# Seven block products in place of eight for two pairs of column chunks in each of ten gated FFNs

## The chip, the cores and the metric

One core of a Trainium2 chip runs the whole program. The metric is device time in microseconds (us), the median of the runs. The engines are named as in the profile: PE is TensorE (matrix products; PEld are its weight loads), DVE is VectorE, ACT is ScalarE, POOL is GpSimd, and SP is SyncE, whose queue issues the large transfers from DRAM. Each engine runs its own queue of instructions in order, and waits at an instruction whose inputs, or whose destination buffer, are not free yet.

## The reference

A network of 256 tokens with 1024 features, all in float32: four layers of FFN, attention, FFN, and then two layers of a mixer and an FFN. What the change touches are the ten FFNs, eight of the first kind and two of the second (`modulate` scales and shifts by columns of a small product with `w_ada`):

```python
D_MODEL = 1024; SEQ = 256; DEPTH = 4; DEPTH_2 = 2; D_FF = 2816

def swiglu(x, w_in, w_out):
    gate, up = jnp.split(x @ w_in, 2, axis=-1)
    return (jax.nn.silu(gate) * up) @ w_out

h = h + 0.5 * rms_norm(swiglu(rms_norm(h, g[0]), ffn_w_in[i, 0], ffn_w_out[i, 0]), g[1])
...
mod = c_act @ w_ada[l] + b_ada[l]
```

The weights of the FFNs come from DRAM in float32, and each is used once.

## The kernel before, in words

**Products.** A float32 value is split into two float32r parts, hi and lo. `hilo` does it: ACT casts a tile to hi (line 168) and DVE subtracts hi from the tile to give lo (line 169). `mm3` then takes a product as three PE matmuls of 128x512, xh·wh, xh·wl and xl·wh (lines 217, 219, 221), accumulated in a PSUM bank. `weights` loads a raw tile of 128x2048 (1 MB) on SP's queue (line 179) and splits it in two halves of 128x1024. There are 2 raw buffers (`RAW_BUFS`) and 9 buffers each for hi and lo (`W_BUFS`).

**An FFN.** The tokens are two tiles of 128 (t = 0, 1), the 1024 features are 8 k-tiles, and the 2816 hidden columns are 11 chunks of 256. `f1(c, t)` takes chunk c's gate and up columns side by side (512 columns): four hi/lo pairs per chunk, and per token tile a *first product* of 8 k-tiles × 3 = 24 matmuls. `hidden` then makes the hidden values: tanh on ACT (line 411), two DVE operations (lines 413 and 414) into the tile `hd`, and two PE transposes (line 249), whose result ACT and DVE split again into `hT` (lines 261, 262). `f2(c, t)` multiplies `hT` with chunk c's rows of `w_out` (two hi/lo pairs, 12 matmuls of 128x512) and accumulates in the banks `aA` or `aB`. A chunk is thus 48 + 24 matmuls of 128x512 on PE, and six hi/lo pairs on ACT and DVE.

**Order.** `ffn` issues the first products of chunks 0 and 1, and then for each chunk c two first products and the second products of chunk c − 2. `middle` (after chunk 3) loads the gain of the norm, or in the second block starts a task that sums a gate (`gbc`). After each of chunks 4 to 7 `ada_step` adds 256 rows of `w_ada`, weighted, to a tile `ada`: four DVE operations of 128x512 on a raw tile of its own, `araw` (lines 1027, 1029). Chains that hop between engines are generators, which are continued when a clock counted in matmuls reaches their time; the list of instructions that comes of this is then put on the engines' queues by the framework's scheduler, once and for all, when the program is built.

In the text the FFNs are numbered #1 to #10 in order of time, and *the stretch* of an FFN runs from the end of its fourth first product (chunks 0 and 1 for both token tiles) to the start of the first product of chunk 8. Chunks 2 to 7 lie in it, so both changed pairs do.

Of the kernel before, what the change touches and what calls it, by code (L numbers as in the profile page):

```python
# [37 lines left out]
W_BUFS = 9  # L38
# [3 lines left out]
GATE_STEP = 9.0  # L42

# [56 lines left out]
class _Net:  # L100
# [63 lines left out]
    # A float32 value is the exact sum of two float32r parts, hi and lo.  x @ w is taken as  # L164
    # xh @ wh + xh @ wl + xl @ wh, accumulated in float32.
# [75 lines left out]
    def last_steps(self, acc, steps):  # L241
        """steps: (hT, ws); one half of the columns after the other"""
# [8 lines left out]
    def to_hT(self, nat, scale=None):  # L251
        """[128 tok, 256] -> (hi, lo) [128, 2, 128 tok]."""
# [16 lines left out]
    def setup(self):  # L269
# [13 lines left out]
        def columns(src, rows, eng=nc.sync):  # L283
            """DRAM [rows, 128] -> [128, rows]."""
# [21 lines left out]
    def mean_square(self, halves, a0, a1):  # L306
        """a0 + a1 * the sum of squares of two [128, 512]; a1 is a number, a0 a number or [128, 1]"""
# [56 lines left out]
    def post_norm(self, t, acc, g_bc, a=1.0, eps=EPS):  # L364
        """h += acc * (a * mean square of acc + eps) ^ -1/2 * g"""
# [17 lines left out]
    def prepare(self, n, t):  # L383
        """Starts what the next part of the network needs of a token tile."""
# [12 lines left out]
    def ffn(self, w_in, w_out, factors, finish, middle):  # L397
        """factors(t): r / 2 and r^2 for x's factor r, which x^T lacks; finish(t, acc) takes the
        accumulated product, in which the hidden values are r^2 (1 + tanh(r g / 2)) g u."""
# [30 lines left out]

        first = ((0, 0), (0, 1), (1, 0), (1, 1)) if self.stage == 0 else ((0, 0), (1, 0), (0, 1), (1, 1))
        for c, t in first:
            f1(c, t)
        for c in range(2, NCH):
            for t in range(NT):
                f1(c, t)
                if c < NCH - 1:
                    f2(c - 2, t=t)
            if c == 3:
                middle()  # L440
            elif self.stage > 0 and c in (4, 5, 6, 7):
                self.ada_step()
# [4 lines left out]
        self.drain()  # L447

    def ffn_1(self, li, j):
# [14 lines left out]
        self.ffn(self.a["ffn_w_in"][li, j], self.a["ffn_w_out"][li, j], factors, finish, middle)  # L464

# [1 line left out]
    def rope(self, x, nh, t):  # L467
        """first 16 of 64 dims of nh heads of x [128, nh, 64], in place"""
# [24 lines left out]
    def softmax(self, s, n, l):  # L493
        """s: PSUM [128, n, l] -> exp(s/8 - max) [128, n, l] and sums [128, n]"""
# [21 lines left out]
    def masked_scores(self, parts, dg):  # L516
        """parts: (psum slice, q^T, k^T) of a bank; dg: psum [128, n, 128], the diagonal blocks"""
# [11 lines left out]
    def qkv_layer(self, kind, w_in, w_out, li):  # L529
        """diff (kind 0) or plain causal (kind 1: with 256 tokens the one block of 256 is every  # L530
        query's own and none is left to select) attention."""
# [38 lines left out]
        def heads(j, t, pairs, last):  # L570
            """A group of pairs of 64-wide heads (or of diff heads of 2 components)."""
# [884 lines left out]
```

## Time and profile before

| | us |
|---|---|
| runs | 2875.92, 2868.54, 2875.60 |
| median of the runs | 2875.6 |
| the profiled execution's span | 2868.0 |
| PE busy | 2823.5 (98%) |
| PEld busy | 2311.4 (81%) |
| DVE busy | 1879.8 (66%) |
| ACT busy | 1509.0 (53%) |
| POOL busy | 231.5 (8%) |

The page gives the span of the profiled execution and no other time for it; the fastest of the runs is 0.5 above that span, the median 7.6 above it. "Busy" is the time in which an instruction of the engine was under way. Matrix products overlap each other, so that the distance from the start of one to the start of the next is shorter than the time shown for one; the same holds, by less, on DVE, and a duration that is to be added up is therefore read here from start to start.

### The profile page before, as it was taken

How to read it: one execution, taken by the hardware profiler on the slowest of the kernel's cores; microseconds unless marked ns; L12 is line 12 of the kernel's file. 1: busy time of each engine (PE TensorE's matmuls, PEld its weight loads, DVE VectorE, ACT ScalarE, POOL GpSimd, SP SyncE). 2: the span in 40 equal slices, each digit the busy share in tenths (PEclk: the TensorE clock that was granted, in tenths of full speed). 3: DMA queues.
4: the chain of work that ended last, by engine and by line, in shares of the span. 5: the costliest groups of instructions: out<-in, count | busy, mean ns of one | idle time of the engine just before them, and what ended most of it. 6: DMA issues, size and time to landing. Idle time of an engine off the chain costs nothing.

```text
span 2868.0 us, 36025 instructions
## 1 busy us (share of the span) xinstructions
PE 2823.5 (98%) x13373; PEld 2311.4 (81%) x13373; DVE 1879.8 (66%) x2913; ACT 1509.0 (53%) x2655; POOL 231.5 (8%) x441
## 2 busy tenths in 40 slices
PE   8999999999999999999999999999999999999998
PEld 6887788888888888878888888778778888788787
DVE  6565767656466765656767666675676686675854
ACT  5456644545664454557545546654545544554543
POOL 0011200101110010020100001110001000000000
PEclk9999999999999999999999999999999999999999
DMA  7554567555446755552666555365565586564753
GB/s 236 186 181 157 171 219 243 179 188 187 157 158 217 249 182 180 191 157 74 222 211 220 194 181 188 128 227 191 187 203 201 172 294 202 192 223 168 236 182 126
DMA packets 356755, 549.32 MB, mean 192 GB/s; under 512 B 13890, under 2 KB 270772, under 8 KB 356580
## 3 DMA queue, kind: packets, MB, share of 16 engines
q1 hardware_dynamic: 354964, 542.00, 57.5%
q0 software_dynamic: 1248, 4.41, 0.4%
q8 instruction: 105, 1.72, 0.2%
q14 instruction: 70, 0.57, 0.1%
q10 hardware_dynamic: 368, 0.62, 0.1%
HBM read 545.93 MB, written 1.05 MB: 191 GB/s over the span
## 4 chain that ended last, share of the span: by engine, by line
PE 84%; ACT 4%; DVE 4%; DMA 4%; POOL 2%; issue 1%; SPq 0%; POOLq 0%; ACTq 0%; DVEq 0%
PE mm L221 18%; PE mm L217 17%; PE mm L219 17%; PE aA L217 4%; PE aA L219 4%; PE aA L221 4%; PE tp L249 4%; PE aB L221 3%; PE aB L217 3%; PE aB L219 3%; DVE lo L169 2%; ACT hi L168 1%; DMA raw<-in_ffn_w_in_dram 1%; DMA raw<-in_w_in_dram 1%; ACT junk L312 1%
## 5 line engine op out<-in xcount | busy, mean ns | idle before, releaser
L169 DVE TENSOR_TENSOR lo<-raw,hi 128x1024 fp32r<-128x1024 f32 x914 | 1102.1, 1221 | 668.1 <-ACT hi L168 655.7
L168 ACT CAST hi<-raw 128x1024 fp32r<-128x1024 f32 x914 | 942.8, 1049 | 927.6 <-PE mm L221 318.9
L217 PE MATMUL mm<-hi,xh 128*128 128x512 f32 (+2 forms) x2496 | 1005.2, 403 | 5.7 <-ACT hi L168 4.0
L221 PE MATMUL mm<-hi,xl 128*128 128x512 f32 (+2 forms) x2496 | 976.7, 392 | 4.3 <-DVE xl L352 4.3
L219 PE MATMUL mm<-lo,xh 128*128 128x512 f32 (+2 forms) x2496 | 973.0, 390 | 0.5 <-DVE lo L169 0.5
L221 PEld LDWEIGHTS mm<-hi,xl 128*128 128x128 f32 x2496 | 469.0, 188 | 108.6 <-DVE xl L352 8.1
L217 PEld LDWEIGHTS mm<-hi,xh 128*128 128x128 f32 x2496 | 469.7, 188 | 94.0 <-ACT hi L168 4.4
L219 PEld LDWEIGHTS mm<-lo,xh 128*128 128x128 f32 x2496 | 470.6, 189 | 87.6 <-DVE lo L169 1.0
L217 PE MATMUL aA<-hi,hT 128*128 128x512 f32 x584 | 194.1, 397 | 2.3 <-DVE on L631 2.3
L219 PE MATMUL aA<-lo,hT 128*128 128x512 f32 x584 | 190.6, 390 | 0.0
L221 PE MATMUL aA<-hi,hT 128*128 128x512 f32 x584 | 190.1, 391 | 0.0
L217 PE MATMUL aB<-hi,hT 128*128 128x512 f32 x568 | 188.8, 395 | 0.0
L221 PE MATMUL aB<-hi,hT 128*128 128x512 f32 x568 | 185.7, 390 | 0.8 <-DVE hT L265 0.8
L219 PE MATMUL aB<-lo,hT 128*128 128x512 f32 x568 | 186.0, 390 | 0.0
L313 POOL TENSOR_SCALAR s<-s 128x1 f32<-128x1 f32 x58 | 35.5, 611 | 1401.6 <-ACT junk L312 1400.9
L262 DVE TENSOR_TENSOR hT<-tp,hT 128x256 fp32r<-128x256 f32 x268 | 111.3, 419 | 27.0 <-ACT hT L261 26.1
L221 PEld LDWEIGHTS aA<-hi,hT 128*128 128x128 f32 x584 | 109.6, 188 | 23.4
L217 PEld LDWEIGHTS aA<-hi,hT 128*128 128x128 f32 x584 | 108.2, 188 | 24.6 <-issue 3.4
L219 PEld LDWEIGHTS aA<-lo,hT 128*128 128x128 f32 x584 | 109.7, 188 | 22.6
L261 ACT CAST hT<-tp 128x256 fp32r<-128x256 f32 x268 | 97.2, 367 | 55.7 <-PE tp L249 55.2
L221 PEld LDWEIGHTS aB<-hi,hT 128*128 128x128 f32 x568 | 106.6, 188 | 24.0 <-DVE hT L265 1.2
L217 PEld LDWEIGHTS aB<-hi,hT 128*128 128x128 f32 x568 | 106.4, 188 | 22.9 <-ACT P L503 1.3
(250 smaller groups left out, 2444.6 us busy)
## 6 DMA issues: line engine op xcount, KB each, us to landing
raw<-in_ffn_w_in_dram SPq DMA_DIRECT2D x352, 512.0 KB, 4.9
raw<-in_ffn_w_out_dram SPq DMA_DIRECT2D x88, 1024.0 KB, 5.0
raw<-in_w_in_dram SPq DMA_DIRECT2D x44, 1024.0 KB, 5.2
raw<-in_w_ffn_in_dram SPq DMA_DIRECT2D x88, 512.0 KB, 5.0
araw<-in_w_ada_dram SPq DMA_DIRECT2D x40, 1024.0 KB, 5.6
raw<-in_w_ffn_out_dram SPq DMA_DIRECT2D x22, 1024.0 KB, 5.0
raw<-in_diff_w_in_dram SPq DMA_DIRECT2D x32, 512.0 KB, 4.5
raw<-in_nsa_w_in_dram SPq DMA_DIRECT2D x9, 1024.0 KB, 5.1
```

Of the source, the lines that this page charges most:

```text
L168: self.nc.scalar.copy(hi, raw)
L169: self.nc.vector.tensor_tensor(lo, raw, hi.bitcast(F32), op=ALU.subtract)
L217: mm(ps, xh[k], wh[:, c], start=first, stop=False)
L219: mm(ps, xh[k], wl[:, c], start=False, stop=False)
L221: mm(ps, xl[k], wh[:, c], start=False, stop=last)
L249: self.nc.tensor.transpose(dst, src, self.ident[:k, :k])
L261: nc.scalar.copy(hi, v)
L262: nc.vector.tensor_tensor(lo, v, hi.bitcast(F32), op=ALU.subtract)
L312: nc.scalar.activation(junk, halves[i], AF.Square, accum_out=ss[:, i : i + 1])
L313: nc.gpsimd.tensor_scalar(v[:, 0:1], ss[:, 0:1], a1, a0, op0=ALU.mult, op1=ALU.add)
```

## The change

Chunks 3 and 4 are taken together, and chunks 6 and 7; the others stay as they were (`PLAN`). For such a pair the first products are a 2x2 block product: two token tiles, by two halves of the 1024 features, by two chunks. It is done by Strassen's scheme with seven products of half as many k-tiles (`seven`): a *block product* is 4 k-tiles × 3 = 12 matmuls of 128x512, and seven of them are 84 matmuls where there were 96. Here the 512 columns of a block are one chunk pair's gate columns or up columns.

- The four blocks of weights come as 1 MB transfers into four buffers `rs` (line 442), are summed in place by DVE (line 461, 128x1024), and each of the seven sums is split anew: 14 hi/lo pairs per pair of chunks where there were 8.
- The seven combinations of x are made once per FFN (`halves_of_x`): x is put together from its parts (line 559), in the first eight FFNs multiplied by the norm's factor per token (line 561, from two small PE products), summed (lines 566 to 572) and split into `Sh` and `Sl`.
- The block products are combined by DVE out of PSUM and in `sc` and `res` tiles (line 461, 128x512), with ACT copies (line 466); tanh and the three operations that give the hidden values now run on 512 columns (lines 471, 472, 475).
- The buffers of hi and lo go from 9 to 7 each, and `ada_add` takes the weights' raw buffers where it had its own tile in the FFNs.

```diff
-W_BUFS = 9
+W_BUFS = 7
...
+PLAN = ((0, 1), (1, 1), (2, 1), (3, 2), (5, 1), (6, 2), (8, 1), (9, 1), (10, 1))
...
+        def seven(c):
...
+            S = sums["S"]
+            raw = {}
+            for k, n in ((0, 0), (1, 0), (0, 1), (1, 1)):
+                raw[k, n] = self.t(self.mp, [P, 4, 512], "rs", bufs=4)
+                nc.sync.dma_start(raw[k, n], self.cols(w_in, c * FC + n * DFF, 512, 4 * k, 4))
+
+            def block(i, r, other=None):
+                ps = self.ps("mm")
+                ws = []
+                for q in range(2):
+                    v = r[:, 2 * q : 2 * q + 2]
+                    if other is not None:
+                        add(v, v, other[:, 2 * q : 2 * q + 2])
...
+                    self.hilo(v, hi, lo)
+                    ws += [(hi[:, j], lo[:, j]) for j in range(2)]
+                x = ([S[0][:, i, k] for k in range(4)], [S[1][:, i, k] for k in range(4)])
+                for k in range(4):
+                    self.mm3([(ps, slice(0, 512))], x, k, ws[k], k == 0, k == 3)
+                return ps
...
+            s = tile(block(0, raw[0, 0]))
+            g0 = self.t(self.fp, [P, 512], "res", bufs=2)
+            add(g0, block(1, raw[1, 0]), s)
+            gate(g0)
+            u1 = tile(block(3, raw[0, 0], raw[0, 1]))
+            pop()
+            add(s, block(4, raw[0, 0], raw[1, 1]), s)
+            u0 = tile()
+            add(u0, s, u1)
+            add(u0, block(6, raw[1, 1]), u0)
+            self.start(out(0, g0, u0))
+            pop()
+            add(s, block(5, raw[0, 1], raw[1, 1]), s)
+            add(u1, s, u1)
+            pop()
+            add(s, block(2, raw[0, 0], raw[1, 0]), s)
+            gate(s)
+            self.start(out(1, s, u1))
+            pop()
...
-        for c in range(2, NCH):
-            for t in range(NT):
-                f1(c, t)
-                if c < NCH - 1:
-                    f2(c - 2, t=t)
-            if c == 3:
+        self.start(self.halves_of_x(sums, scaled))
+        done, ada = 2, 0
+        for c, n in PLAN[2:]:
+            if n == 2:
+                self.force(lambda: "S" in sums)
+                seven(c)
+            else:
...
+            while self.stage > 0 and ada < min(4, done - 4):
+                ada += 1
                 self.ada_step()
...
+    def halves_of_x(self, res, scaled):
...
+        f = self.t(self.mp, [P, 4, 512], "rs", bufs=4)
...
         src = self.cols(self.a["w_ada_2"][l], i * D, D, 2 * u, 2)
-        if self.stages[self.stage]["attention"]:
-            raw = self.t(self.wp, [P, 2 * UW], "raw", bufs=RAW_BUFS)
-        else:
-            raw = self.t(self.mp, [P, 2 * UW], "araw", bufs=1)
+        raw = self.t(self.wp, [P, 2 * UW], "raw", bufs=RAW_BUFS)
```

**The queues.** The diff leaves the order on each queue to the scheduler, so it is shown here for FFN #3. Lines 169, 217, 219, 221, 179, 262 and 1029 of the kernel before are lines 172, 220, 222, 224, 182, 265 and 1155 after. DVE before, at the first products of chunk 3 (`mm` is a PSUM bank, `fs` the norm's factor, the number at a name tells tiles apart):

```order
L169 TENSOR_TENSOR lo_5168<-raw_5164,hi_5167 128x1024
L169 TENSOR_TENSOR lo_5172<-raw_5164,hi_5171 128x1024
L262 TENSOR_TENSOR hT_5068<-tp_5064,hT_5067 128x256
L169 TENSOR_TENSOR lo_5179<-raw_5175,hi_5178 128x1024
L413 SCALAR_TENSOR_TENSOR hd_5088<-th_5086,mm_5054 128x256
L414 SCALAR_TENSOR_TENSOR hd_5088<-hd_5088,fs_1086_4581,mm_5054 128x256
L169 TENSOR_TENSOR lo_5183<-raw_5175,hi_5182 128x1024
L262 TENSOR_TENSOR hT_5127<-tp_5123,hT_5126 128x256
L169 TENSOR_TENSOR lo_5226<-raw_5223,hi_5225 128x1024
L169 TENSOR_TENSOR lo_5230<-raw_5223,hi_5229 128x1024
L413 SCALAR_TENSOR_TENSOR hd_5147<-th_5145,mm_5113 128x256
L414 SCALAR_TENSOR_TENSOR hd_5147<-hd_5147,fs_1100_4671,mm_5113 128x256
```

DVE after, inside the first seven, at the third and fourth of the block products (`rs_5214`, `rs_5218` and `rs_5220` are three of the four blocks of weights, `raw_5303` is a tile of `w_out`):

```order
L461 TENSOR_TENSOR rs_5214<-rs_5214,rs_5218 128x1024
L265 TENSOR_TENSOR hT_5244<-tp_5240,hT_5243 128x256
L461 TENSOR_TENSOR rs_5214<-rs_5214,rs_5218 128x1024
L172 TENSOR_TENSOR lo_5281<-rs_5214,hi_5280 128x1024
L461 TENSOR_TENSOR res_5252<-mm_5253,sc_5250 128x512
L172 TENSOR_TENSOR lo_5286<-rs_5214,hi_5285 128x1024
L472 SCALAR_TENSOR_TENSOR res_5252<-res_5275,res_5252 128x512
L172 TENSOR_TENSOR lo_5306<-raw_5303,hi_5305 128x1024
L172 TENSOR_TENSOR lo_5310<-raw_5303,hi_5309 128x1024
L461 TENSOR_TENSOR rs_5214<-rs_5214,rs_5220 128x1024 x2
L461 TENSOR_TENSOR rs_5218<-rs_5218,rs_5220 128x1024
L172 TENSOR_TENSOR lo_5328<-rs_5214,hi_5327 128x1024
```

Before, a hi/lo pair per 12 matmuls and two half-width operations per product were all that stood there; now block sums of the full 128x1024 stand between the pairs, and sums of 128x512 take results from PSUM. In the whole program PE has 7152 matmuls of 128x512 in place of 7392, and DVE has 160 block sums, 120 lo's of 128x1024, 302 other sums or lo's and 100 more operations of the form with a scalar on 128x512 that it had not, and 160 operations of 128x256 fewer.

SP before, the loads for chunks 4 and 5 and the rows of `w_out` between them:

```order
L179 DMA raw_5301<-in_ffn_w_in_dram 128x4x256 x2
L179 DMA raw_5312<-in_ffn_w_in_dram 128x4x256 x2
L179 DMA raw_5360<-in_ffn_w_out_dram 128x2x1024
L179 DMA raw_5437<-in_ffn_w_in_dram 128x4x256 x2
L179 DMA raw_5448<-in_ffn_w_in_dram 128x4x256 x2
L179 DMA raw_5496<-in_ffn_w_out_dram 128x2x1024
```

SP after, from the last `w_out` tile in the first seven to the loads of chunk 5 and beyond (`raw_5504` and `raw_5633` are rows of `w_ada`; `raw_5510` and `raw_5521` are the two halves of chunk 5's gate and up columns, `rs_5639` to `rs_5645` the blocks of the second seven):

```order
L182 DMA raw_5425<-in_ffn_w_out_dram 128x2x1024
L1147 DMA raw_5504<-in_w_ada_dram 128x2x1024
L442 DMA rs_5639<-in_ffn_w_in_dram 128x4x512
L442 DMA rs_5641<-in_ffn_w_in_dram 128x4x512
L182 DMA raw_5510<-in_ffn_w_in_dram 128x4x256 x2
L442 DMA rs_5643<-in_ffn_w_in_dram 128x4x512
L182 DMA raw_5521<-in_ffn_w_in_dram 128x4x256 x2
L182 DMA raw_5562<-in_ffn_w_out_dram 128x2x1024
L442 DMA rs_5645<-in_ffn_w_in_dram 128x4x512
L1147 DMA raw_5633<-in_w_ada_dram 128x2x1024
```

The blocks of the second seven now stand ahead of the loads of chunk 5. There are four `rs` buffers, taken in turn; the fourth tile back from `rs_5639` in that turn is `rs_5214`, whose buffer it takes. DVE after, at the end of the first seven:

```order
L172 TENSOR_TENSOR lo_5450<-rs_5214,hi_5449 128x1024
L461 TENSOR_TENSOR rs_5214<-rs_5214,rs_5216 128x1024
L1153 TENSOR_SCALAR ada_5503<-raw_5504,col_213_884 128x512 x2
L1155 SCALAR_TENSOR_TENSOR ada_5503<-raw_5504,col_213_884,ada_5503 128x512
L172 TENSOR_TENSOR lo_5455<-rs_5214,hi_5454 128x1024
L1155 SCALAR_TENSOR_TENSOR ada_5503<-raw_5504,col_213_884,ada_5503 128x512
L172 TENSOR_TENSOR lo_5514<-raw_5510,hi_5513 128x1024
L461 TENSOR_TENSOR sc_5250<-mm_5447,sc_5250 128x512
L172 TENSOR_TENSOR lo_5518<-raw_5510,hi_5517 128x1024
```

The last reader of `rs_5214` is `lo_5455`, and two rows behind it stands `lo_5514`, the first lo of chunk 5, which needs `raw_5510`.

## Rows read from the trace of the kernel before

**Rows 1.** The profile's page, parts 1 and 2: engines over the whole span, and the granted clock.

```profile
PE 2823.5 (98%) x13373; PEld 2311.4 (81%) x13373; DVE 1879.8 (66%) x2913; ACT 1509.0 (53%) x2655; POOL 231.5 (8%) x441
...
PEclk9999999999999999999999999999999999999999
```

**Rows 2.** Windows: one stretch of each FFN, #1, #3, #9, #10, and all ten.

```profile
core 0: us, PE busy (x) PEld busy (x) DVE busy (x) ACT busy (x) POOL busy (x), PEclk, DMA share, GB/s
38.00:141.60 103.60, 103.36 (x465) 83.33 (x464) 61.92 (x88) 48.38 (x64) 1.85 (x2) 1.00 0.60 194
...
542.20:643.20 101.00, 101.00 (x457) 83.00 (x456) 60.02 (x77) 47.34 (x62) 1.85 (x2) 1.00 0.57 181
...
2302.00:2403.90 101.90, 101.90 (x460) 83.73 (x459) 77.18 (x105) 47.68 (x65) 3.21 (x3) 1.00 0.78 262
2695.80:2797.80 102.00, 102.00 (x462) 83.78 (x461) 67.47 (x89) 47.30 (x64) 0.00 (x0) 1.00 0.65 216
sum 1014.60, PE 1014.36 PEld 831.73 DVE 657.83 ACT 479.05 POOL 14.68; mean PE 101.44 PEld 83.17 DVE 65.78 ACT 47.91 POOL 1.47
```

**Rows 3.** Groups by line, FFN #3's stretch (busy us, mean ns, idle before).

```profile
L169 DVE TENSOR_TENSOR lo<-raw,hi 128x1024 fp32r<-128x1024 f32 x37 | 44.8, 1224 | 37.7 <-ACT hi L168 37.0
...
L168 ACT CAST hi<-raw 128x1024 fp32r<-128x1024 f32 x36 | 37.2, 1049 | 43.6 <-PE mm L221 23.3 <-DMA raw<-in_ffn_w_in_dram 20.2
```

**Rows 4.** Waits, FFN #3's stretch (us in total, times, longest).

```profile
ACT hi L168 <- DMA raw<-in_ffn_w_in_dram: 20.2, 10, 4.9
```

**Rows 5.** Timeline, the stretch's start (start, us, engine, line, what).

```profile
542.24 0.47 ACT L411 ACTIVATE th<-mm,fs 128x256 f32<-128x256 f32 x1 [0.33 <-PE mm L221]
...
543.19 0.41 DVE L413 SCALAR_TENSOR_TENSOR hd<-th,mm 128x256 f32<-128x256 f32 x1
```

**Rows 6.** Timeline, PE inside the stretch.

```profile
601.06 0.39 PE L217 MATMUL mm<-hi,xh 128*128 128x512 f32 x1
601.28 0.39 PE L219 MATMUL mm<-lo,xh 128*128 128x512 f32 x1
```

**Rows 7.** Timeline, DVE, three places.

```profile
187.93 0.42 DVE L262 TENSOR_TENSOR hT<-tp,hT 128x256 fp32r<-128x256 f32 x1
188.26 0.41 DVE L413 SCALAR_TENSOR_TENSOR hd<-th,mm 128x256 f32<-128x256 f32 x1
...
197.21 1.41 DVE L379 SCALAR_TENSOR_TENSOR res<-aA,s,gbc 128x512 f32<-128x512 f32 x2 [4.49 <-POOL s L304]
198.53 1.28 DVE L380 TENSOR_TENSOR h<-h,res 128x512 f32<-128x512 f32 x2
199.74 1.22 DVE L169 TENSOR_TENSOR lo<-raw,hi 128x1024 fp32r<-128x1024 f32 x1
...
561.01 2.36 DVE L169 TENSOR_TENSOR lo<-raw,hi 128x1024 fp32r<-128x1024 f32 x2 [2.81 <-ACT hi L168]
```

**Rows 8.** Transfers: page part 6 (KB, us to landing), SP's timeline, GB/s over 0:45.

```profile
raw<-in_ffn_w_in_dram SPq DMA_DIRECT2D x352, 512.0 KB, 4.9
raw<-in_ffn_w_out_dram SPq DMA_DIRECT2D x88, 1024.0 KB, 5.0
...
542.96 0.92 SPq L179 DMA_DIRECT2D raw<-in_ffn_w_in_dram  x2
546.41 0.37 SPq L179 DMA_DIRECT2D raw<-in_ffn_w_out_dram  x1
...
GB/s 0 59 251 267 354 393 382 368 350 347 379 378 216 22 185 344 378 279 331 376 103 0 38 269 347 390 318 322 171 24 51 317 426 138 164 281 383 118 150 296
```

**Rows 9.** Timeline, PE at the program's first products.

```profile
11.91 0.79 PE L217 MATMUL mm<-hi,xh 128*128 128x512 f32 x1 [3.99 <-ACT hi L168]
...
14.18 0.63 PE L217 MATMUL mm<-hi,xh 128*128 128x512 f32 x1
14.61 0.63 PE L219 MATMUL mm<-lo,xh 128*128 128x512 f32 x1
...
16.20 0.40 PE L221 MATMUL mm<-hi,xl 128*128 128x512 f32 x1
```

More of the change, by code (lines that the diff above doesn't have):

```diff
@@ L394, in prepared, with ffn @@
         return self.ready[self.stage, t]
-    def ffn(self, w_in, w_out, factors, finish, middle):
+    def ffn(self, w_in, w_out, factors, finish, middle, scaled):
         nc = self.nc
@@ L429, in f2, with add, tile, gate @@
                 self.out_step(acc[t], *steps[0], cs[0] == 0, False)
+        def seven(c):
[11 more added lines that the diff above has]
+                        add(v, v, other[:, 2 * q : 2 * q + 2])
+                    hi = self.t(self.wp, [P, UW], "hi", F32R).rearrange("p (a b) -> p a b", a=2)
+                    lo = self.t(self.wp, [P, UW], "lo", F32R).rearrange("p (a b) -> p a b", a=2)
+                    self.hilo(v, hi, lo)
[4 more added lines that the diff above has]
+                return ps
+            def add(dst, u, v):
+                nc.vector.tensor_tensor(dst, u, v, op=ALU.add)
+            def tile(ps=None):
+                r = self.t(self.mp, [P, 512], "sc", bufs=3)
+                if ps is not None:
+                    nc.scalar.copy(r, ps)
+                return r
+            def gate(g):
+                th = self.t(self.fp, [P, 512], "res", bufs=2)
+                nc.scalar.activation(th, g, AF.Tanh, scale=0.5)
+                nc.vector.scalar_tensor_tensor(g, th, 1.0, g, op0=ALU.add, op1=ALU.mult)
+            def out(t, g, u):
+                nc.vector.scalar_tensor_tensor(u, g, -1.0, u, op0=ALU.mult, op1=ALU.mult)
+                yield 2.0
+                for i in range(2):
+                    hT[c + i, t] = self.to_hT(u[:, FC * i : FC * i + FC])
+            s = tile(block(0, raw[0, 0]))
[17 more added lines that the diff above has]
+            pop()
+            queue.extend((c + i, t) for i in range(2) for t in range(NT))
@@ L431, in ffn, with pop @@
+        queue, sums = [], {}
+        def pop():
+            c, t = queue.pop(0)
+            f2(c, t=t)
         first = ((0, 0), (0, 1), (1, 0), (1, 1)) if self.stage == 0 else ((0, 0), (1, 0), (0, 1), (1, 1))
@@ L433, in ffn @@
             f1(c, t)
-        for c in range(2, NCH):
-            for t in range(NT):
-                f1(c, t)
-                if c < NCH - 1:
-                    f2(c - 2, t=t)
-            if c == 3:
+        queue.extend((c, t) for c in range(2) for t in range(NT))
+        self.start(self.halves_of_x(sums, scaled))
[5 more added lines that the diff above has]
+            else:
+                for t in range(NT):
+                    f1(c, t)
+                    queue.append((c, t))
+                    if c < NCH - 1:
+                        pop()
+            done = c + n
+            if done > 3 and middle:
                 middle()
-            elif self.stage > 0 and c in (4, 5, 6, 7):
+                middle = None
+            while self.stage > 0 and ada < min(4, done - 4):
+                ada += 1
                 self.ada_step()
@@ L447, in ffn, with put @@
         self.drain()
+    def halves_of_x(self, res, scaled):
+        nc = self.nc
+        if not scaled:
+            fs = [self.prepared(t) for t in range(NT)]
+            rb = self.t(self.mp, [P, NT, P], "rb")
+            ps = self.ps("tp")
+            for t in range(NT):
+                nc.tensor.matmul(ps[:, t * P : t * P + P], fs[t][:, 0:1].to_broadcast([P, P]), self.ident,
+                                 start=True, stop=True)
+            nc.scalar.copy(rb, ps[:, :S].rearrange("p (a b) -> p a b", a=2))
+        S_ = [self.t(self.mp, [P, 7, 4, P], f"S{n}", F32R) for n in "hl"]
+        def put(i, v):
+            self.hilo(v, S_[0][:, i], S_[1][:, i])
+        f = self.t(self.mp, [P, 4, 512], "rs", bufs=4)
+        x = {}
+        for t in (0, 1):
+            for k in (0, 1):
+                xh, xl = (v[:, 4 * k : 4 * k + 4].bitcast(F32) for v in self.xT[t])
+                v = x[t, k] = f[:, 2 * t + k].rearrange("p (a b) -> p a b", a=4)
+                nc.vector.tensor_tensor(v, xh, xl, op=ALU.add)
+                if not scaled:
+                    nc.vector.tensor_tensor(v, v, rb[:, t, None, :].to_broadcast([P, 4, P]), op=ALU.mult)
+        tt, stt = nc.vector.tensor_tensor, nc.vector.scalar_tensor_tensor
+        put(0, x[0, 0])
+        put(1, x[0, 1])
+        put(2, x[1, 1])
+        tt(x[1, 1], x[1, 1], x[1, 0], op=ALU.subtract)
+        put(3, x[1, 1])
+        tt(x[1, 0], x[0, 0], x[1, 0], op=ALU.subtract)
+        put(5, x[1, 0])
+        stt(x[0, 0], x[1, 1], -1.0, x[0, 0], op0=ALU.mult, op1=ALU.subtract)
+        put(4, x[0, 0])
+        stt(x[0, 1], x[0, 0], -1.0, x[0, 1], op0=ALU.mult, op1=ALU.subtract)
+        put(6, x[0, 1])
+        res["S"] = S_
+        return
+        yield
     def ffn_1(self, li, j):
@@ L462, in finish @@
             self.post_norm(t, acc, g[0], 4.0, 16.0 * EPS)
-        self.ffn(self.a["ffn_w_in"][li, j], self.a["ffn_w_out"][li, j], factors, finish, middle)
+        self.ffn(self.a["ffn_w_in"][li, j], self.a["ffn_w_out"][li, j], factors, finish, middle, False)
     def rope(self, x, nh, t):
@@ L1133, in ffn_2 @@
         self.ffn(self.a["w_ffn_in_2"][l], self.a["w_ffn_out_2"][l], lambda t: (0.5, 1.0),
-                 lambda t, acc: self.gate_finish(g[0])(t, acc), lambda: g.append(self.start_gate(l, 5)))
+                 lambda t, acc: self.gate_finish(g[0])(t, acc), lambda: g.append(self.start_gate(l, 5)), True)
     def rotary(self, ps, t):
```

## The prediction

> **What bounds the kernel now.** I read the page first. PE is busy in 98% of the span, at the full granted clock in all forty slices, DVE in 66% [rows 1]. An average over stages doesn't tell what a stage is bound by, so next I cut out the stretch of each FFN in which the change works. The windows show that it lasts 103.6 in #1, 101.0 to 101.1 in #2 to #8 (the row of #3 stands for these seven), 101.9 in #9 and 102.0 in #10, and that PE is busy in practically all of it: 1014.36 of 1014.60 [rows 2]. DVE is busy in 60.02 of #3's 101.00. Its idle time is spent in front of lo's whose hi ACT has not made yet, 37.0 [rows 3], and ACT in turn waits 20.2 for raw tiles [rows 4]. None of this is felt, since PE always finds a finished pair. So PE sets the pace today, and in these stretches DVE has about 40 to spare.
>
> How much of that slack the change takes is the question, and for it DVE's lead at the start of the stretch matters. There is next to none: DVE's `hd` of the fourth product needs that product from PE, and starts at 543.19, 1.0 after the product ended at 542.2, with tanh on ACT between [rows 5]. What stands behind it on DVE's queue can't have begun earlier. So the stretch can't be shorter than this 1.0 plus the DVE work from that `hd` to the first lo of chunk 8. I counted it on DVE's queue after the change.
>
> **What it removes.** A stretch has 432 matmuls of 128x512 before and 408 after, in ten stretches 240 fewer. Matmuls follow each other in 0.227 (601.06, 601.28 and on [rows 6]), so PE is spared 24 × 0.227 = 5.4 per stretch, 54.5 in all. The two small products for the norm's factor cost back some 0.2 per FFN. PE alone would need 101.0 − 5.4 = 95.6.
>
> **What it adds on DVE.** Prices go from start to start, in rows where nothing waits: two operations of 128x512 with a scalar take 197.21 to 198.53, 0.66 each; two without, 198.53 to 199.74, 0.60 each; an `hT` 187.93 to 188.26, 0.33; a pair of lo's of 128x1024 lasts 2.36, less the 1.22 of one, so 1.14 [rows 3, 7]. The two operations of an `hd` get 0.9, twice the 0.41 of the first and a little [rows 5]. The trace has no sum of two 128x1024 tiles in place. Below it lies the 0.60 of half its size, above it twice that, 1.20; I take the lo's 1.14, the same operation with the same number of elements. Over 160 of them the ends would make the sum 86 lower or 10 higher; the range takes them in. For sums out of PSUM I take 0.60 too.
>
> In #2 to #8, each: 46 lo's × 1.14 = 52.4; 16 block sums × 1.14 = 18.2; 27 operations with two tensors on 128x512 × 0.60 = 16.2; 10 with a scalar × 0.66 = 6.6; 16 of `ada` × 0.66 = 10.6; five pairs for `hd` × 0.9 = 4.5; 11 `hT` × 0.33 = 3.6. Sum 112.1, with the 1.0 ahead 113.1, against 101.0: **+12.1** each, 85 for seven. (`ada` stands outside #3's stretch before; now four steps of it lie in each of #2 to #9.) #1 has no `ada` and no lo of it, one sum and one scalar operation less: 100.1 against 103.6, −3.5. #9 has its x sums ahead of the stretch, but the 16 operations of a gate and three more lo's inside: 119.3 against 101.9, +17.4. #10 the same without `ada`: 105.6 against 102.0, +3.6. Together 84.7 − 3.5 + 17.4 + 3.6 = **+102**.
>
> A rule of the Trainium skill speaks of these prices. The trace has lo's of 1.22 follow each other in 1.14 [rows 3, 7]. The page "VectorE: DVE Perf Modes", section "The DRAIN you can't avoid", says that the next operation does not start until the pipe is empty. By it each would cost its whole duration, some 0.08 more for about 130 operations of a stretch, an estimate of 10 per stretch and 100 in the sum below; the trace shows the overlap, so I keep to it.
>
> **What it adds in waits.** Once DVE sets the end, its waits count. One is plain from the queues. SP issues the blocks `rs_5639` and `rs_5641` ahead of `raw_5510`, and `rs_5639` takes the buffer of `rs_5214`, which is read until `lo_5455`. So chunk 5's weights are asked for when DVE has finished the first seven, and two rows later DVE wants `lo_5514`. Between lies one `ada` operation, 0.66. Ahead of the lo, 3 MB are to come. One 1 MB tile lands 5.0 after its issue; issues take SP 0.37 for one transfer of 1 MB and 0.92 for a tile of two halves [rows 8]. If the three were carried at once: 0.37 × 2 + 0.92 + 4.9 + 1.05 for the hi − 0.66 = 7.0 of idle DVE; one after another 3 × 5.0 + 1.05 − 0.66 = 15.4. The fastest slices of the first 45 us move some 380 GB/s [rows 8], or 2.8 per MB; 5.0 + 2 × 2.8 + 1.05 − 0.66 gives 11, nearer to the rows than either end. PE has only the last six matmuls of the block (1.4) to cover it. Ten FFNs: **+109** (10.9 each; 70 to 154). (1.05 is ACT's cast [rows 3].)
>
> Smaller waits of this kind follow, since weights of `w_out`, `ada` and chunk 8 share two raw buffers: a tile is 5.0 + 1.05 away when its buffer is let go, and DVE has 4.3, 5.5 and 5.7 of other work there: 1.8 + 0.6 + 0.4 if nothing else is in the way; I take 2 per FFN, **+20** (0 to 40). W_BUFS from 9 to 7 costs nothing: the cover is DVE itself, which is late and finds buffers free. Without that cover PE would wait for pairs in the other chunks; I leave it at 0, up to 10 in the range. ACT has 47.34 of work in #3's stretch [rows 2]; nine more hi's and the copies leave it below 75.
>
> After such a gap PE's clock may matter. In the trace PE waits 3.99 at the program's start, and its first matmuls then follow each other in 0.43, until the ninth at 16.20 [rows 9]: eight times 0.2, or 1.6. If that came back behind each of ten gaps it would be 16. From these rows alone I take 0, since two lo's (2.3) stand between the product's last pair and the `hd` that waits for it; 16 goes into the range. The Trainium skill, "TensorE: Matmul & The Clock Gate", section "HAM oscillation — how this bites in real kernels", says that bursts of products with waits between fall back to the lower clock each time. By it the sum would be 3115, an estimate from the 16 above; the granted clock is 1.00 in every window here [rows 2], and no run here has such a gap in its middle.
>
> **The sum.** 102 + 109 + 20 = 231, on 2868.0: **3099**. That is against the profiled execution; the median of the runs lies 7.6 higher, the lowest 0.5, so I give 3100.
>
> **Rivals.**
> *DVE keeps ahead and PE's saving comes through.* Then 2868 − 54.5 + 2 = 2816. It decides where the DVE work of a stretch is below PE's 95.6, 17 less than I count. For it speaks that DVE has 40 idle there today [rows 2]; against it that the added work is 52 and the lead is cut to 0 by `hd`. 3%.
> *The blocks' wait is hidden*, because the block is let go earlier or the loads land in time: 2868 + 102 + 20 = 2990. For it: a raw tile's wait of 20.2 is hidden today [rows 4]. Against it: the order on SP's queue. 13%.
> *The waits lie at their upper bounds:* 2868 + 102 + 154 + 40 + 16 = 3180. For it: DMA is at 0.57 to 0.78 of its time in the stretches already [rows 2]. 12%.
> *The clock stays at half through the stretch:* 408 × 0.43 = 175 and some 3 for the rest, 50 over my 127 in each, 3099 + 500 = 3600. PE would be idle for a quarter of the stretch, but mostly in one gap. 1%.
> *No change:* excess and saving would have to cancel; 1%. That the change doesn't do what it says is excluded by the count of matmuls.
>
> **How the numbers follow.** My forecast has 70%. Its own range is 3040 to 3160, from the waits' bounds. The range reaches to the hidden wait and the upper bounds: 2970 to 3180. About 0.3%, or 9 us, is what can be told from no change: faster 0.03, same 0.01, slower 0.96.
>
> **What would show it.** Right: #2 to #8's stretches at 124 to 130, PE busy for three quarters of them; DVE busy for about 2380 (1880, and by the counts of the whole program 280 × 1.14 + 302 × 0.60 + 100 × 0.66 − 160 × 0.4 = 502); one wait of about 11 in front of chunk 5's first hi, on its raw tile, in every FFN; PE waiting for lo's inside both sevens. Wrong: stretches near 96 with a busy PE (the first rival), stretches at 113 with no such wait (the second), or matmuls 0.43 apart behind the gap (the fourth).

## The result

The changed kernel takes 3069.98 us, the median of four runs (3065.42 to 3074.60); the kernel before, beside it, 2874.56 (2868.54 to 2875.92). The ratio is 1.0685, with a 95% interval of 1.0668 to 1.0702: slower, by some 195 us. The profiled execution has a span of 3070.1, against 2868.0, so 202 more. (The traces have 10976 float32 matmuls of 128x512 before and 10736 after. The totals 7392 and 7152 given ahead of the prediction are wrong; their difference of 240, with which it reckons, is right.)

The page of the changed kernel, parts 1, 2 and 5:

```profile
span 3070.1 us, 36361 instructions
...
PE 2883.0 (94%) x13165; PEld 2282.6 (74%) x13165; DVE 2362.9 (77%) x3435; ACT 1668.3 (54%) x2853; POOL 228.5 (7%) x441
...
PEclk9999999999999999999999999999999998999999
...
L461 DVE TENSOR_TENSOR rs<-rs,rs 128x1024 f32<-128x1024 f32 x160 | 190.1, 1216 | 0.0
```

PE is no longer busy throughout, and DVE has gone from 66% to 77% [rows 1]. The granted clock has one slice under nine tenths. A block sum, for which the trace before had only bounds, lasts 1216 ns, as long as a lo.

The stretches (windows as in [rows 2], with the same columns; #1, #3, #9, #10, and the sum over all ten):

```profile
38.50:146.50 108.00, 103.23 (x443) 80.08 (x442) 102.53 (x135) 60.35 (x83) 0.00 (x0) 0.98 0.43 148
...
566.60:681.60 115.00, 102.54 (x440) 78.17 (x438) 110.23 (x137) 60.23 (x79) 0.37 (x1) 0.98 0.50 168
...
2459.60:2588.50 128.90, 104.83 (x437) 79.22 (x435) 116.53 (x144) 56.60 (x74) 0.54 (x1) 0.96 0.54 185
2886.70:2997.90 111.20, 102.68 (x430) 80.35 (x429) 103.62 (x123) 55.24 (x71) 0.00 (x0) 0.95 0.50 170
sum 1162.70, PE 1032.82 PEld 791.12 DVE 1095.73 ACT 594.28 POOL 1.46; mean PE 103.28 PEld 79.11 DVE 109.57 ACT 59.43 POOL 0.15
```

DVE now is the busy engine, 110.23 of 115.00 in #3. In all ten stretches it is busy in 1095.73 of 1162.70, so it stands idle in 67; before, it was busy in 657.83 of 1014.60 [rows 2] and idle in 357. PE has pauses now. "PE busy" flatters it: the time shown for a matmul covers part of its neighbour's, and short pauses vanish in it. Where the parts of an FFN begin and end can be read from the first and last matmuls of its products. Here they are summed over the program, for all kernels of this study. Each row is one profiled execution; those of late_ada and one_pair are the longest of their runs, 11.6 and 6.8 above the medians.

```
                    stretches   last chunks   starts   between    span
                    (4th first  (chunk 8 to   of FFNs  FFNs
                     product to  last first
                     chunk 8)    product)
before                 1014.5       460.5      246.8    1121.0   2868.0
after                  1162.6       485.9      257.2    1139.9   3070.1
no_sums                 990.1       475.9      254.5    1145.0   2890.2
late_ada               1062.0       553.7      257.7    1167.4   3065.9
one_pair               1110.8       474.6      255.1    1137.0   3002.3
w7                     1015.2       460.6      255.2    1139.2   2895.1
before_raw             1031.0       465.2      246.9    1125.2   2893.0
one_rs                 1056.4       463.7      254.6    1137.0   2936.2
pool_sums              1314.3       476.8      255.1    1138.7   3209.5
late_rs                1046.1       478.4      255.3    1144.2   2949.3
filler                 1171.2       478.1      254.1    1139.4   3067.4
filler28               1175.9       472.1      257.3    1137.2   3067.1
w7_raw                 1030.8       467.1      254.4    1142.4   2919.6
late_rs_no_sums         972.3       466.6      255.3    1142.3   2861.5
```

What a row lacks to its span, about 25, is the end of the program. Of the 202 more, 148 lie in the stretches, 25 in the last chunks, and 29 at the starts of FFNs and between them. So most of the loss is where it was forecast, but 54 is not.

**The wait that was forecast isn't there.** SP's queue and DVE's around the end of FFN #3's first seven (start, us, engine, line, what; the first three rows are SP's):

```profile
606.09 3.80 SPq L442 DMA_DIRECT2D rs<-in_ffn_w_in_dram  x2
613.26 0.92 SPq L182 DMA_DIRECT2D raw<-in_ffn_w_in_dram  x2
616.10 0.37 SPq L442 DMA_DIRECT2D rs<-in_ffn_w_in_dram  x1
```

```profile
604.81 1.22 DVE L461 TENSOR_TENSOR rs<-rs,rs 128x1024 f32<-128x1024 f32 x1
...
608.28 1.22 DVE L172 TENSOR_TENSOR lo<-rs,hi 128x1024 fp32r<-128x1024 f32 x1
...
614.85 1.22 DVE L461 TENSOR_TENSOR rs<-rs,rs 128x1024 f32<-128x1024 f32 x1
...
617.44 1.22 DVE L172 TENSOR_TENSOR lo<-rs,hi 128x1024 fp32r<-128x1024 f32 x1
618.58 0.75 DVE L1155 SCALAR_TENSOR_TENSOR ada<-raw,col,ada 128x512 f32<-128x512 f32 x1
619.90 1.23 DVE L172 TENSOR_TENSOR lo<-raw,hi 128x1024 fp32r<-128x1024 f32 x1 [0.58 <-ACT hi L171]
```

The two blocks of the second seven are issued from 606.09 on, the first of them right behind the block sum that began at 604.81 and ended at 606.03, long before the last lo of the first seven at 617.44. So `rs_5639` doesn't wait for that lo. The second issue of that row comes 3.80 − 0.37 later, at 609.52, when the lo from 608.28 is done, and the third block's at 616.10, when the sum from 614.85 is done: each time a block of the first seven has just been read for the last time. So the buffers are not taken in turn, as the text ahead of the prediction has it, but in the order in which they come free. Chunk 5's tile is asked for at 613.26. DVE waits 0.58 for it, not 11. In the whole stretch DVE waits 2.5 for hi's, and ACT 2.2 for these tiles:

```profile
DVE lo L172 <- ACT hi L171: 2.5, 5, 0.6
ACT hi L171 <- DMA raw<-in_ffn_w_in_dram: 2.2, 2, 1.6
```

### The profile page after: what moved, and what is told of

Read it like the earlier page. It is cut to its first block, busy times and chain, and to the rows that moved or that the text cites. A ratio compares the mean times of both kernels' runs of the same rounds, so it can differ in the third digit from the quotient of the medians.

```text
span 3070.1 us, 36361 instructions
## 1 busy us (share of the span) xinstructions
PE 2883.0 (94%) x13165; PEld 2282.6 (74%) x13165; DVE 2362.9 (77%) x3435; ACT 1668.3 (54%) x2853; POOL 228.5 (7%) x441
## 4 chain that ended last, share of the span: by engine, by line
PE 57%; DVE 25%; DMA 7%; ACT 6%; issue 3%; POOL 2%; SPq 0%; ACTq 0%; POOLq 0%; DVEq 0%
DVE lo L172 12%; PE mm L222 12%; PE mm L224 11%; PE mm L220 11%; DVE rs L461 4%; PE aA L220 3%; PE tp L252 3%; DMA raw<-in_ffn_w_in_dram 3%; ACT hi L171 3%; PE aA L222 3%; PE aA L224 3%; PE aB L220 2%; PE aB L224 2%; PE aB L222 2%; DVE sc L461 2%
## 5 line engine op out<-in xcount | busy, mean ns | idle before, releaser
L172 DVE TENSOR_TENSOR lo<-raw,hi 128x1024 fp32r<-128x1024 f32 x754 | 904.9, 1219 | 323.7 <-ACT hi L171 315.4
L220 PE MATMUL mm<-hi,xh 128*128 128x512 f32 (+2 forms) x1856 | 753.2, 409 | 22.9 <-ACT hi L171 19.2
L222 PE MATMUL mm<-lo,xh 128*128 128x512 f32 (+2 forms) x1856 | 734.0, 398 | 9.9 <-DVE lo L172 8.9
L224 PE MATMUL mm<-hi,xl 128*128 128x512 f32 (+2 forms) x1856 | 729.2, 395 | 5.5 <-DVE xl L355 5.3
L171 ACT CAST hi<-rs 128x1024 fp32r<-128x1024 f32 x280 | 284.0, 1048 | 232.8 <-DVE rs L461 217.0
L172 DVE TENSOR_TENSOR lo<-rs,hi 128x1024 fp32r<-128x1024 f32 x280 | 333.3, 1217 | 5.0 <-ACT hi L171 4.7
L220 PE MATMUL mm<-hi,Sh 128*128 128x512 f32 x560 | 230.3, 411 | 26.8 <-ACT hi L171 26.2
L222 PE MATMUL mm<-lo,Sh 128*128 128x512 f32 x560 | 227.7, 407 | 21.1 <-DVE lo L172 20.9
L224 PE MATMUL mm<-hi,Sl 128*128 128x512 f32 x560 | 223.3, 399 | 0.0
L220 PE MATMUL aA<-hi,hT 128*128 128x512 f32 x584 | 199.2, 405 | 13.8 <-ACT hi L171 12.6
L461 DVE TENSOR_TENSOR rs<-rs,rs 128x1024 f32<-128x1024 f32 x160 | 190.1, 1216 | 0.0
```

The costliest lines, as they stand in the source:

```text
L171: self.nc.scalar.copy(hi, raw)
L172: self.nc.vector.tensor_tensor(lo, raw, hi.bitcast(F32), op=ALU.subtract)
L220: mm(ps, xh[k], wh[:, c], start=first, stop=False)
L222: mm(ps, xh[k], wl[:, c], start=False, stop=False)
L224: mm(ps, xl[k], wh[:, c], start=False, stop=last)
L461: nc.vector.tensor_tensor(dst, u, v, op=ALU.add)
```

## The experiments

The theory after the result: in the stretches DVE's work sets the pace. The rivals: each pair has a cost of its own (chains of sum, hi, lo and product, waits for its blocks); the shared raw buffers or the fewer hi/lo buffers; PE's clock behind pauses.

**late_ada**

```diff
-            while self.stage > 0 and ada < min(4, done - 4):
+            while self.stage > 0 and ada < min(4, 2 * (done - 8)):
```

> The four steps of the w_ada sums come after chunks 8 and 9 of an FFN, not inside the stretch; nothing else changes. If DVE's work sets the length of the stretch: it loses 13 us of work there in #2 to #9 (111.0 to 97.9 by the queue's rows), PE needs 95.2, so these stretches fall from 115 to 119 (129 in #9) to 102 to 106, and the time by about 90 to 105, to some 2965 to 2980. If the transfers or the two raw buffers set it (the same loads go through the same buffers, only later): by less than 20, 3050 or more.

Measured: 3056.33, ratio 1.0644 (1.0618 to 1.0670). The time is the rival's, the stretches are the theory's: 102.7 to 106.8 in #2 to #8, 111.6 in #9. FFN #3's stretch and last chunks:

```profile
566.50:672.40 105.90, 100.82 (x436) 79.49 (x435) 100.83 (x120) 60.52 (x80) 0.00 (x0) 0.98 0.43 148
672.40:732.10 59.70, 53.49 (x212) 41.76 (x210) 42.77 (x60) 21.94 (x31) 1.85 (x2) 0.89 0.67 212
```

Taking work from DVE shortens the stretch by nearly as much as the work (100.6 less in ten, for eight times 13). The loads of these rows left the stretch too; but in #3 DVE's busy time fell by 9.4 and the stretch by 9.1, while its idle time stayed at 5, so what the stretch lost is the work. The last chunks grew by 68, though, and the parts between the FFNs by 27. In #3's last chunks neither PE (at a clock of 0.89) nor DVE is full. Two waits of that window:

```profile
ACT hi L171 <- DMA raw<-in_ffn_w_in_dram: 7.3, 4, 3.1
...
ACT hi L171 <- DMA raw<-in_ffn_w_out_dram: 4.1, 2, 2.7
```

So the shared raw buffers came under suspicion; late_rs below decides.

**no_sums**

```diff
-                        add(v, v, other[:, 2 * q : 2 * q + 2])
+                        pass
```

> The sums of weight blocks are left out (each block product takes the first block unsummed, so the products are others); loads, splits, products and all other sums stay. If DVE's work sets the stretch: 16 x 1.14 = 18 fewer on DVE, 92.1 against PE's 95.2, stretches of 97 to 100, and 2875 to 2900 in all. If waits for transfers, buffers or the longer chains set it: a saving below 60, 3010 or more.

Measured: 2890.47, ratio 1.0064 (1.0050 to 1.0078), as the theory says. The stretch of #3:

```profile
539.40:637.10 97.70, 97.15 (x436) 78.68 (x434) 91.39 (x120) 60.88 (x79) 0.00 (x0) 1.00 0.60 199
```

PE is full again, and 16 operations of DVE fewer took 17.3 from this stretch, 172 from all. The edit also shortens the chain from block to product, so by itself it doesn't tell DVE's work from that rival; late_ada does, since its steps stand in no such chain.

**one_pair**

```diff
-PLAN = ((0, 1), (1, 1), (2, 1), (3, 2), (5, 1), (6, 2), (8, 1), (9, 1), (10, 1))
+PLAN = ((0, 1), (1, 1), (2, 1), (3, 2), (5, 1), (6, 1), (7, 1), (8, 1), (9, 1), (10, 1))
```

> Only chunks 3 and 4 are a pair; 6 and 7 are single. If DVE's work sets the stretch: with one pair DVE has 91.4 and PE 98.1, so PE is the bound again and the stretches come to 98 to 100; the time falls to 2850 to 2890, next to the kernel before (2868 to 2876), though half of the pairs remain. If each pair costs by itself (waits for its blocks, chains of sums between PE, ACT and DVE): half of the 195 remains, about 2970.

Measured: 2997.20, ratio 1.0437 (1.0419 to 1.0455). Both missed, the theory by over 100. #3's stretch, cut at the first product of chunk 5:

```profile
559.60:614.60 55.00, 51.89 (x218) 40.07 (x218) 52.70 (x69) 29.73 (x41) 0.00 (x0) 0.97 0.34 117
614.60:671.20 56.60, 53.26 (x231) 41.16 (x230) 39.81 (x53) 24.52 (x34) 1.13 (x2) 1.00 0.74 234
```

The sum over the stretch had hidden two stages. In the first DVE is full (52.70 of 55.00), in the second it isn't, and the time that it has to spare there doesn't help the first. So the bound has to be taken per stage, also inside a stretch. The second stage, three single chunks, takes 56.6; before, these three took 50.6.

**w7, before_raw, w7_raw**: the kernel before with one side part of the change, the other, and both.

```diff
-W_BUFS = 9
+W_BUFS = 7
```

```diff
-        if self.stages[self.stage]["attention"]:
-            raw = self.t(self.wp, [P, 2 * UW], "raw", bufs=RAW_BUFS)
-        else:
-            raw = self.t(self.mp, [P, 2 * UW], "araw", bufs=1)
+        raw = self.t(self.wp, [P, 2 * UW], "raw", bufs=RAW_BUFS)
```

> The kernel before with W_BUFS = 7 in place of 9. The theory: the buffers cost nothing inside the FFNs (stretches stay at 101.0) and about 8 in the attention between FFN #5 and #6 and 10 in the other parts between FFNs, so 2880 to 2895. Rival: they cost inside the FFNs too, 2900 or more; or nothing anywhere, 2868 to 2876.

> The kernel before, with one part of the change alone: the rows of w_ada go through the weights' two raw buffers in the FFNs too (W_BUFS stays 9). In the run with one pair the single chunks with such a step took 18.6 to 19.4 us in place of 16.9. If the shared buffers do that by themselves, 32 steps cost up to 2 us each: stretches of #2 to #9 at 103 to 109, 2890 to 2935 in all. If it takes a DVE or ACT without any lead, nothing is seen here, where PE has finished pairs in hand: stretches at 101, 2868 to 2880.

> The kernel before with both side parts of the change, W_BUFS = 7 and the rows of w_ada through the raw buffers, and no pair. They cost 26 and 24 alone. If they add up: 2915 to 2925, and the pairs themselves cost the other 145 to 155. If they meet in the same places: 2895 to 2910. If fewer buffers make the shared raw buffers worse: 2930 or more.

Measured: w7 2896.83, 1.0096 (1.0081 to 1.0112); before_raw 2894.80, 1.0084 (1.0070 to 1.0098); w7_raw 2919.97, 1.0167 (1.0153 to 1.0181). They add up, as the theory has it. w7 came 2 above its range. before_raw's time is in its range, but six of its eight stretches, at 101.0 to 102.4, lie below theirs. The fewer buffers cost nothing in the stretches and 27 at the starts and between FFNs (the table), which is nearly all that the changed kernel loses there; through which waits is not shown, nor what nine buffers would do in the changed kernel. The shared buffers cost up to 2.3 in the ordinary stretches, and 10.4 in #9, where `ada` and a gate go through them:

```profile
2312.30:2424.60 112.30, 107.48 (x464) 85.87 (x463) 74.14 (x104) 43.06 (x61) 0.00 (x0) 0.97 0.67 217
```

That is 112.3 with no pair in it, against 101.9 [rows 2].

**one_rs**

```diff
-        raw = self.t(self.wp, [P, 2 * UW], "raw", bufs=RAW_BUFS)
+        if self.stages[self.stage]["attention"]:
+            raw = self.t(self.wp, [P, 2 * UW], "raw", bufs=RAW_BUFS)
+        else:
+            raw = self.t(self.mp, [P, 4, 512], "rs", bufs=4).rearrange("p a b -> p (a b)")
```

with the `PLAN` of one_pair.

> One pair (3 and 4), and the rows of w_ada go through the pair's own four buffers, which are free behind the pair, in place of the weights' raw buffers. If the shared raw buffers slow the single chunks 5 to 7: these three go from 56.6 back to 51 to 53, and the time from 2997 to 2955 to 2970. If it is that they start without a lead: 2990 to 3004 as before. The stretch's first part, to the start of chunk 5, stays at 54 to 55 in both cases, since DVE has the same work there.

Measured: 2938.90, ratio 1.0238 (1.0224 to 1.0252), 58 under one_pair. #3's stretch, cut in the same way:

```profile
553.40:606.10 52.70, 50.18 (x213) 39.12 (x211) 50.99 (x66) 29.48 (x41) 0.00 (x0) 0.97 0.47 160
606.10:659.10 53.00, 52.58 (x235) 42.73 (x236) 44.40 (x59) 27.24 (x36) 1.85 (x2) 1.00 0.69 225
```

The time is 16 below the forecast. The cut here falls at a matmul of chunk 5 that stands ahead of the pair's last five; cut behind those, at 607.6, as in one_pair, the parts are 54.2 (DVE busy in 52.49) and 51.5. So the single chunks are back near the 50.6 of before, and the first stage is nearly as long as in one_pair. Both hold: shared buffers in the second stage, DVE's work in the first. With one pair these buffers alone cost 58, where before_raw has 24 for them.

**late_rs**: late_ada's line and one_rs's buffers, with both pairs.

> Both pairs, the steps of w_ada after chunks 8 and 9 as in late_ada, and their rows through the pairs' four buffers, which are free by then. In late_ada the stretches lost what was forecast, but the last three chunks grew from 49 to 55 to 60. If the shared raw buffers made them grow: they come to 47 to 51, the stretches stay at 103 to 106, and the time falls to 2960 to 2985. If it was DVE, which has 44 of work there and starts without a lead: still 54 to 58, and 3040 to 3060.

Measured: 2952.84, ratio 1.0284 (1.0268 to 1.0299), 117 under the changed kernel.

```profile
552.50:655.60 103.10, 99.21 (x435) 78.11 (x435) 98.84 (x119) 60.29 (x79) 0.00 (x0) 1.00 0.54 182
655.60:702.30 46.70, 46.70 (x212) 37.97 (x211) 42.09 (x59) 22.63 (x31) 1.86 (x2) 1.00 0.68 226
```

The stretches are even shorter than in late_ada, #3's last chunks are at 46.7, and the parts between the FFNs are 23 shorter than there. What undid late_ada's gain was the shared buffers. The time came 7 below the forecast.

**filler, filler28**

```diff
+                if i == 2 and c == 6:
+                    d = self.ps("tp")
+                    for n in range(16):
+                        nc.tensor.matmul(d, x[0][3], ws[3][0], start=n == 0, stop=n == 15)
```

and with 28 in place of 16. They come from this piece of PE's timeline in the changed kernel, between the last block product of #3 and chunk 8:

```profile
674.64 0.39 PE L224 MATMUL mm<-hi,Sl 128*128 128x512 f32 x1
679.48 1.09 PE L252 MATMUL tp<-cst,sc 128*128 128x128 f32 x4 [4.45 <-DVE sc L475]
681.56 1.22 PE L220 MATMUL mm<-hi,xh 128*128 128x512 f32 x2 [1.00 <-ACT hi L171]
...
684.27 0.63 PE L222 MATMUL mm<-lo,xh 128*128 128x512 f32 x1
684.69 0.63 PE L224 MATMUL mm<-hi,xl 128*128 128x512 f32 x1
...
686.67 0.39 PE L224 MATMUL mm<-hi,xl 128*128 128x512 f32 x1
686.90 0.40 PE L220 MATMUL mm<-hi,xh 128*128 128x512 f32 x1
```

PE pauses 4.45 and 1.00, and its next matmuls stand 0.42 apart (684.27, 684.69), until they are back at 0.23 at 686.67. The granted clock, over the last chunks and over their first 4.8 us (0.50 is the lower of its two levels, 1.2 of 2.4 GHz):

```profile
681.60:730.40 48.80, 48.76 (x207) 39.05 (x208) 34.01 (x44) 25.41 (x33) 1.48 (x2) 0.95 0.64 209
681.60:686.40 4.80, 4.76 (x10) 3.27 (x11) 2.99 (x4) 3.39 (x5) 1.48 (x2) 0.50 0.55 148
```

> Sixteen more matmuls of 128x512 that nothing reads, with the last block product of the second seven, where PE has 4.5 us and more to wait. If the half clock behind that wait is what makes the three last chunks 48 to 49.5 long in place of 45 to 46: they fall to 46 to 47, and the time by 15 to 25, to 3045 to 3055, although PE has 36 us more to do in all. If it is the missing lead of DVE: nothing gained, 3065 to 3080, or longer by the fillers' 3.6 us per FFN, up to 3106.

> Twenty-eight fillers in place of sixteen, twenty-two of them behind the last block product, so that PE is busy almost until chunk 8's weights are there. With sixteen it still paused 1.8 and 1.3 and began chunk 8 at half clock. If the clock is what the last three chunks lose: they fall to 46.2 to 46.8 at a granted clock of 1.00, against 48 to 49.5. If the lead is: 47.5 to 49 as with sixteen. The time itself: 3045 to 3070, since the fillers can also hold up the last transposes.

Measured: filler 3068.30, 1.0692 (1.0677 to 1.0706); filler28 3069.33, 1.0697 (1.0680 to 1.0714). Sixteen left pauses of 1.8 and 1.3 and the half clock behind them. With 28 chunk 8 began at the full clock, and the last chunks of #3 took 47.3 at 1.00:

```profile
687.70:735.00 47.30, 46.74 (x207) 37.71 (x208) 34.18 (x44) 25.29 (x33) 1.59 (x2) 1.00 0.67 217
```

That doesn't decide between the two: it lies between 46.8 and 47.5. In the whole program 13.8 of the 25 lost in the last chunks came back. Of these 11.5 lie in #2 to #8, where the half clock at chunk 8 is gone, and 2.0 in #1 and #10, where chunk 8 began at the full clock in both kernels; #9, where the half clock stayed, gained nothing. So the half clock costs about 1.6 in the last chunks of each of seven FFNs. The fillers held up the stretches by as much as came back (13.3), so nothing was gained in time. For what remains there are only hints: w7_raw, without a pair, loses 6.6 in the last chunks, and in one_rs they are 10.9 shorter than in one_pair, by nothing but the buffers of `ada`'s rows.

**pool_sums**

```diff
-                        add(v, v, other[:, 2 * q : 2 * q + 2])
+                        nc.gpsimd.tensor_tensor(v, v, other[:, 2 * q : 2 * q + 2], op=ALU.add)
```

> The sixteen sums of weight blocks of an FFN go to GpSimd, in place of DVE; everything is still computed. DVE then has 92.8 in the stretch against PE's 95.2. If DVE's work is the bound and GpSimd takes under 3 us for a sum, 97 to 104 for the stretch and 2890 to 2960. If the chain from sum to hi to lo to product is what counts, or the two engines hold each other up, no better than 3070.

Measured: 3210.84, ratio 1.1185 (1.1170 to 1.1201). The window of #3's stretch, and groups by line of GpSimd and of DVE in it:

```profile
597.60:729.00 131.40, 105.62 (x434) 81.29 (x433) 125.42 (x120) 60.41 (x79) 48.23 (x16) 0.95 0.44 149
...
L450 POOL TENSOR_TENSOR rs<-rs,rs 128x1024 f32<-128x1024 f32 x16 | 48.2, 3025 | 76.3 <-DVE lo L172 40.8 <-PE aB L224 31.6 <-ACT sc L466 3.6
...
L172 DVE TENSOR_TENSOR lo<-rs,hi 128x1024 fp32r<-128x1024 f32 x28 | 54.9, 1990 | 0.0
L172 DVE TENSOR_TENSOR lo<-raw,hi 128x1024 fp32r<-128x1024 f32 x16 | 24.9, 1568 | 2.2 <-ACT hi L171 2.2
...
L461 DVE TENSOR_TENSOR sc<-mm,sc 128x512 f32<-128x512 f32 x8 | 5.4, 681 | 1.5 <-PE mm L224 1.5
```

A sum takes 3.0 there, and DVE's lo's have gone from 1.22 to 1.99 for the blocks and 1.57 for the other tiles, while its operations with one operand in PSUM (`sc<-mm,sc`) keep their 0.68. DVE is busy in 125.42 of that stretch's 131.40: still the bound, with fewer operations that take longer. The time is the rival's, and of the two causes that it names the rows show that GpSimd holds DVE up.

**late_rs_no_sums**: late_rs without the block sums.

> late_rs, and the sums of weight blocks left out as in no_sums. It asks from which point PE's saving comes through. DVE has 80 in the stretch against PE's 95.2. If DVE's work was what hid the saving: stretches of 95.5 to 98, last chunks of 46 to 47.5, and 2840 to 2860, under the kernel before by the 54 saved less the 26 that W_BUFS = 7 costs between the FFNs. If the block products have a cost of their own (pauses of PE between shorter chains): stretches of 99 or more, 2875 or above.

Measured: 2862.94, ratio 0.9958 (0.9943 to 0.9974): 3 above the theory's range and 0.4% under the kernel before, though the sums it leaves out are part of the method.

```profile
537.40:634.10 96.70, 96.70 (x435) 78.91 (x434) 87.92 (x111) 62.82 (x80) 0.00 (x0) 1.00 0.64 216
```

PE is the bound again, and its saving comes through: 972.3 in ten stretches against 1014.5, 42 of the 54. No kernel with a pair that computes all of it came under the kernel before; the nearest is one_rs.

## Why the prediction was right, and where it was not

The direction, the range and the time (3100 against 3070) hold, but the 225 that were forecast aren't the 195 that were measured, term by term.

- *DVE sets the pace in the stretches: right, and shown.* no_sums and late_ada take 18 and 13 from DVE's queue in a stretch. #3 gets shorter by 17 without the sums, and #2 to #9 by 12 in the mean without the steps of `ada`. For #3 the sum of prices gave 113.1; it took 115.0. The price of a block sum, 1.14, holds, and with it the overlap that the prediction kept to: three sums, each shown as 1.22, take 594.53 to 597.94 in #3, 3.41.

```profile
594.53 3.49 DVE L461 TENSOR_TENSOR rs<-rs,rs 128x1024 f32<-128x1024 f32 x3
597.94 4.62 DVE L172 TENSOR_TENSOR lo<-rs,hi 128x1024 fp32r<-128x1024 f32 x4
```

- *+102 for DVE's work: about right; +20 for small waits: too low.* The 102 are 92 of work beyond the old stretches (1107 in ten, against 1014.5) and 10 for the start. DVE was busy in 1095.73 of the ten stretches, so the work came to 81. Its idle time came to 67, where the sum had 10 + 20 for it beside the blocks' wait. Together the stretches lost 148, 46 more than 102. Some 16 of these may be the shared raw buffers, which is what before_raw shows on the kernel before, mostly in #9; I had priced them by one tile's landing, as if nothing else passed through them. In late_rs, whose stretches have no steps of `ada`, DVE is still idle for 4.3 in #3 (98.84 of 103.10). In #3 of the changed kernel the 4.8 are short waits, 2.5 of them for hi's; no run shows what would take them away.
- *+109 for the blocks' wait: wrong.* The step that failed is "`rs_5639` takes the buffer of `rs_5214`". I took the buffers in the order in which the tiles were made; by the time of its issue it took that of the first block to be done with, the one that the sum from 604.81 read last. DVE waited 0.58 in #3 in place of 10.9, and no wait of DVE in any of the ten stretches is longer than 3.4. On this point the rival with the hidden wait was right; its 2990 is too low for the terms that it shares with my sum.
- *W_BUFS from 9 to 7 "costs nothing": wrong.* 26, outside the stretches, in the starts of FFNs and between them, by w7. I had looked for the cover only where DVE is late, and let the range hold 10.
- *The clock, 0 with up to 16 in the range: about 12.* Not where I looked for it, behind chunk 5's wait, but behind the second seven. The page "TensorE: Matmul & The Clock Gate" of the Trainium skill, section "HAM oscillation — how this bites in real kernels", has bursts behind waits fall to the lower clock; here the trace agrees, at 0.50 behind the pause of 4.45 and 1.00. The other half of what the last chunks lost had no term at all.
- *The first rival's point.* I had it decide where DVE's work falls below PE's 95.6. With DVE busy in 91.39 (no_sums) and 87.92 (late_rs_no_sums) PE is full in #3's stretch, and in late_rs_no_sums 42 of the 54 come through; one_pair shows that the comparison must hold in each stage, not over the stretch.
- *The signs.* #2 to #8 were to take 124 to 130, with PE busy for three quarters. They took 114.9 to 119.4, and PE was busy in 89% of #3's, which is nearer to the second rival's 113. DVE's 2380 over the program came to 2362.9.

So the mechanism in the stretches was right, and that 3100 came near 3070 is luck: 109 for a wait that isn't there and 20 for smaller ones stood in for 46 in the stretches, 25 in the last chunks and 29 at the starts and between the FFNs.

## What to carry to other kernels

Weigh an exchange of one engine's work for another's stage by stage, against what the second engine has left in that very stage. Here 240 matmuls fewer, 54 us of PE, cost 483 us of DVE in the program (1879.8 to 2362.9). DVE had a third of the span idle, but in the ten stretches, where the work came, only 357 of it, and 438 more came to lie there. What a change frees or shares on the side (buffers fewer or in common) belongs in the sum as its own experiment on the kernel before; here two such parts made 48 of 195. Even that can be too little: with one pair, where DVE has less to spare, the shared buffers alone cost 58.

## What the runs showed of the hardware

GpSimd takes 3.0 us in the mean for a sum of two 128x1024 tiles that DVE does in 1.22 (the shortest of pool_sums's 160 takes 2.4), and it holds DVE up: DVE's operations on two SBUF operands went to 1.6 and 2.0, those with one operand in PSUM didn't change. These means mix two kinds. In the whole of pool_sums a lo of a block that no GpSimd sum overlaps still takes 1.21, and the 134 of 280 that one overlaps take 2.74 in the mean. The Trainium skill, "SBUF — State Buffer", section "Who interferes with whom", says that a DVE instruction with two SBUF inputs contends with a GpSimd instruction that reads SBUF; the trace agrees. With 18.2 us of sums taken off it in a stretch, DVE was busy there for 15 more than with them (125.42 against 110.23).
